# Hybrid decoder layer: the first key projection no longer waits for all of the normalizing, with the lead-in and the whole order of work rearranged

## The chip, the cores and the metric

One core of one Trainium2 chip runs the program. The metric is device time in microseconds (us), the median of several executions. The engines are named as in the profile: PE is the matmul engine TensorE (PEld its weight loads), DVE is VectorE, ACT is ScalarE, POOL is GpSimd, SP is SyncE, which here only issues DMAs.

## The reference

512 tokens of width 1024 get 16 learned meta tokens ahead of them, are normalized and projected. One branch is sliding-window attention, the other RWKV-7 time mixing over 16 heads of 64. Both are gated, added, projected, normalized and passed through a squared-ReLU MLP.

```
h = layer_norm(concat([meta, x]), ln0_g, ln0_b)        # 528 x 1024
proj = h @ w_in                                         # 1024 -> 6656 columns
q, k, v, zr, gate_att, gate_rwkv = split(proj)
att = sliding_window_attention(q, k, v, rel_bias, sinks)
z = zr + (previous token's zr - zr) * shift_mu
r, k, v, wl, al, gl = split(z)
w = -softplus(-(w0 + tanh(wl) @ w2)) - 0.5
a = sigmoid(a0 + al @ a2)
S_t = S w_t + (S (-kk_t)) (kk_t a_t)^T + v_t k_t^T ;  y_t = S_t r_t   # per head, over 528 steps
h = layer_norm(ALPHA h + (sigmoid(gate_att) att + sigmoid(gate_rwkv) rw) @ w_out)
out = layer_norm(ALPHA h + square(relu(h @ w_ff1)) @ w_ff2)[16:]
```

## The kernel before

**Operands.** Activations are kept transposed (features on partitions, tokens along the row) and as two tiles, `hhi` (the value rounded to fp32r) and `hlo` (what is left). Weights are split alike into `whi` (ACT, L656) and `wlo` (DVE, L658). A product is three matmuls, hi by hi, lo by hi, hi by lo (L499, L500, L501). A projection of 128 columns takes eight slices of the 1024 features, so 24 of them for the left half of the tokens (columns 0 to 263) and 24 for the right half (262 to 527).

**Lead-in** (`lead`). Four blocks of 128 tokens, x0 to x3, are loaded into `res` tiles (in the order's rows x0 is `res_125`, x1 `res_126`, x2 `res_127`, x3 `res_128`). Mean and variance of a block come from DVE (`stats`: L773, L776 to L778) or from two sums on ACT (`sums`: L790 to L793); POOL takes the power -0.5 (L781, L794). The block is normalized by DVE (L811) or ACT (L803 and L808). PE transposes two blocks at a time, x0 with x1 and then x2 with x3, in four steps each (L844, sixteen records for two blocks). ACT (L852) or DVE (L856) applies gain and bias, ACT writes `hhi` (L860), DVE or POOL writes `hlo` (L862). The meta rows go the same way on a path of their own: ACT L815, PE L821, DVE L829, L830 and L832, ACT L831. `busy` (L733) puts matmuls of the identity in, whose result nobody reads: twenty ahead of the first transposes and eight ahead of the second, by `WARM`. Two more small things are done by PE there: the transpose of the parameter rows (L751) and the table of relative positions (L903).

**Head.** `head` projects the decay and rate inputs (`COL_WA`, tile `zwa` by L873 and L874), the gate's input (`COL_GL`), the attention's keys and values. `shifted` projects one strip and mixes each token with the one before it (L698 on ACT, L701 on DVE). Then comes a loop over eight pairs of heads: `rwkv(j)`, `attention(j)`, `merge(j)`. In `rwkv`, L958 is the first matmul of a pair. Its key strip is projected, L1032 to L1034 take norms of it, L1076 is the scores, POOL solves 32 x 32 blocks by substitution, and L1191, L1196, L1211 and L1227 are small matmuls of one chain, with copies on ACT (L1200 and L1202) and a transposition on DVE (L1198) between them. L1250, L1254 and L1258 are the same for the meta tokens. L1288 is the chain from chunk to chunk (L1270 and L1273 copy its result back). L1342, L1399 and L1411 belong to the attention.

**Order.** Every operation is registered with its reads and writes, which gives its dependencies. What is issued when on which engine is set by the table `ORDER`, a list of the operations' numbers, and `SLOTS`, the buffers that they get. The costs given to `op` (`wire`, `lag`, `port`, the second argument) are for the search that made the table and do nothing on the chip. An operation `whole` depends on all of the lead-in; every matmul group of a projection made after it names it in `after=late`, and so may stand in the table only behind it. Projections made earlier name the parts they need: `parts_in` gives the transposed slices, `cols_in` the parameter columns.

Of the kernel before, what the change touches and what calls it, by code (L numbers as in the profile page):

```python
# [15 lines left out]
ALU = mybir.AluOpType  # L16
# [4 lines left out]
P = 128  # L21
# [4 lines left out]
T = SEQ + NMETA  # L26
# [8 lines left out]
WARM = (20, 8)  # L35
# [41 lines left out]
for _name, _c in ROWS:  # L77
# [177 lines left out]
]  # L255

def _constants():
# [124 lines left out]
def hybrid_layer_kernel(ctx: ExitStack, tc: tile.TileContext, I: dict, out: bass.AP):  # L382
# [330 lines left out]
    def parts_in(s, end):  # L713
        if late:
            return []
# [1035 lines left out]
```

## Time and profile before

| | |
|---|---|
| median of 3 runs | 923.06 us (922.6 to 924.2) |
| the profiled execution | 924.42 us |
| its span, first to last instruction | 922.6 us |
| instructions | 17014 |
| PE busy | 902.2 us, 98% of the span |
| DVE, ACT, POOL busy | 585.8, 456.3, 245.6 us |
| mean granted clock of PE | 0.994 |

A row of the timeline gives start, length, engine, line, operation, what is written and read, shapes, count, and in brackets the idle time before it with what ended it. A row of waits gives who waited for whom, microseconds in total, times, the longest. A row of windows gives a stretch, its length, the busy time of PE, PEld, DVE, ACT and POOL with the counts, the granted clock, the DMA's share and GB/s. `x34` counts records; one matmul call of the identity leaves two. The busy end of a matmul is modelled, so the step from one start to the next tells more than its length.

### The profile page before, as it was taken

How to read it: one execution, taken by the hardware profiler on the slowest of the kernel's cores; microseconds unless marked ns; L12 is line 12 of the kernel's file. 1: busy time of each engine (PE TensorE's matmuls, PEld its weight loads, DVE VectorE, ACT ScalarE, POOL GpSimd, SP SyncE). 2: the span in 40 equal slices, each digit the busy share in tenths (PEclk: the TensorE clock that was granted, in tenths of full speed). 3: DMA queues.
4: the chain of work that ended last, by engine and by line, in shares of the span. 5: the costliest groups of instructions: out<-in, count | busy, mean ns of one | idle time of the engine just before them, and what ended most of it. 6: DMA issues, size and time to landing. Idle time of an engine off the chain costs nothing. (4 is left out here: it accounts for less than half of the span.)

```text
span 922.6 us, 17014 instructions
## 1 busy us (share of the span) xinstructions
PE 902.2 (98%) x6496; PEld 773.6 (84%) x6496; DVE 585.8 (63%) x1141; ACT 456.3 (49%) x1080; POOL 245.6 (27%) x652
## 2 busy tenths in 40 slices
PE   7999999999999999999999999999999999999996
PEld 6999989888998888978878878888888888888885
DVE  7873977868777696587685887864323244442437
ACT  7845568476583664656637448434312234431120
POOL 4147173381634605507537020000000000000001
PEclk9999999999999999999989999999999999999999
DMA  7443323425242242313246322532223232233322
GB/s 265 125 131 99 93 84 101 111 67 127 72 110 86 68 141 69 83 54 114 64 140 182 100 92 69 172 126 92 92 91 107 76 114 92 91 93 98 100 75 92
DMA packets 71370, 95.90 MB, mean 104 GB/s; under 512 B 40071, under 2 KB 47497, under 8 KB 71289
## 3 DMA queue, kind: packets, MB, share of 16 engines
q1 hardware_dynamic: 70448, 93.65, 33.5%
q8 instruction: 51, 0.84, 0.4%
q10 hardware_dynamic: 840, 1.17, 0.3%
q14 instruction: 31, 0.25, 0.1%
HBM read 87.64 MB, written 8.21 MB: 104 GB/s over the span
## 5 line engine op out<-in xcount | busy, mean ns | idle before, releaser
L499 PE MATMUL g<-hhi,whi 128*128 128x512 f32 (+3 forms) x640 | 213.1, 333 | 0.2
L500 PE MATMUL g<-hlo,whi 128*128 128x512 f32 (+3 forms) x640 | 204.1, 319 | 1.7 <-DVE hlo L862 1.7
L501 PE MATMUL g<-hhi,wlo 128*128 128x512 f32 (+3 forms) x640 | 203.6, 318 | 0.0
L476 ACT CAST whi<-wraw 128x512 fp32r<-128x512 f32 x118 | 67.4, 619 | 205.7 <-PE acc L1616 107.4
L479 DVE TENSOR_TENSOR wlo<-wraw,whi 128x512 fp32r<-128x512 f32 x118 | 76.4, 689 | 144.5 <-ACT whi L476 141.7
L499 PEld LDWEIGHTS g<-hhi,whi 128*128 128x128 f32 x640 | 121.0, 189 | 12.6 <-issue 2.2
L500 PEld LDWEIGHTS g<-hlo,whi 128*128 128x128 f32 x640 | 121.2, 189 | 9.7 <-DVE hlo L862 2.1
L501 PEld LDWEIGHTS g<-hhi,wlo 128*128 128x128 f32 x640 | 121.0, 189 | 8.5 <-DVE wlo L658 0.2
L658 DVE TENSOR_TENSOR wlo<-wraw,whi 128x512 fp32r<-128x512 f32 x126 | 88.3, 708 | 30.4 <-ACT whi L656 29.8
L1167 POOL TENSOR_TENSOR ftmp<-Xf,Nf 108x84 f32<-108x84 f32 (+23 forms) x248 | 88.1, 355 | 73.4 <-DMA Nf<-Nd 44.7
L656 ACT CAST whi<-wraw 128x512 fp32r<-128x512 f32 x126 | 76.9, 618 | 55.5 <-PE g L500 23.5
L466 POOL TENSOR_TENSOR rsf<-rsf,mhalf 128x1 f32<-128x1 f32 x4 | 3.9, 964 | 348.5 <-DVE rsf L465 348.5
L1171 POOL TENSOR_TENSOR Xf<-Xf,ftmp 108x84 f32<-108x84 f32 (+23 forms) x248 | 88.5, 357 | 19.0
L1615 PE MATMUL acc<-wlo,fhi 128*128 128x512 f32 x240 | 93.4, 389 | 0.0
L1614 PE MATMUL acc<-whi,fhi 128*128 128x512 f32 x240 | 93.4, 389 | 0.0
L1616 PE MATMUL acc<-whi,flo 128*128 128x512 f32 x240 | 93.4, 389 | 0.0
L501 PE MATMUL dps<-h1hi,wlo 128*128 128x512 f32 x232 | 91.6, 395 | 0.0
L499 PE MATMUL dps<-h1hi,whi 128*128 128x512 f32 x232 | 91.6, 395 | 0.0
L500 PE MATMUL dps<-h1lo,whi 128*128 128x512 f32 x232 | 91.6, 395 | 0.0
L1614 PEld LDWEIGHTS acc<-whi,fhi 128*128 128x128 f32 x240 | 45.0, 188 | 9.5
L1616 PEld LDWEIGHTS acc<-whi,flo 128*128 128x128 f32 x240 | 45.0, 188 | 9.3
L1615 PEld LDWEIGHTS acc<-wlo,fhi 128*128 128x128 f32 x240 | 45.0, 188 | 9.3
(361 smaller groups left out, 1658.4 us busy)
## 6 DMA issues: line engine op xcount, KB each, us to landing
wraw<-in_w_ff_dram SPq DMA_DIRECT2D x64, 512.0 KB
wraw<-in_w_in_dram SPq DMA_DIRECT2D x52, 512.0 KB
wraw<-in_w_out_dram SPq DMA_DIRECT2D x14, 256.0 KB
Nf<-Nd SPq DMA_DIRECT2D x24, 144.0 KB
res<-in_x_dram SPq DMA_DIRECT2D x4, 512.0 KB
G<-in_consts_dram SPq DMA_DIRECT2D x16, 128.0 KB
XB<-xtd SPq DMA_DIRECT2D x16, 128.0 KB
res<-in_x_dram SPq DMA_DIRECT2D x8, 256.0 KB
```

Source lines behind the costliest of these rows:

```text
L476: act.copy(hi[:n, qs], raw[:n, qs])
L479: dve.tensor_tensor(lo[:n, qs], raw[:n, qs], hi[:n, qs].bitcast(F32), op=ALU.subtract)
L499: pe.matmul(ps, whi, xhi, start=first, stop=False)
L500: pe.matmul(ps, whi, xlo, start=False, stop=False)
L501: pe.matmul(ps, wlo, xhi, start=False, stop=last)
L656: AC(512, lambda hi=hi, qs=qs: act.copy(hi.t, raw.t[:, qs]), plain=True, r=[raw], w=[hi], new=[hi])
L658: f = lambda hi=hi, lo=lo, qs=qs, e=e: e.tensor_tensor(lo.t, raw.t[:, qs], hi.t.bitcast(F32), op=ALU.subtract)
L1167: sub(nj * nt, lambda s=s, nj=nj, nt=nt, tv=tv: pool.tensor_tensor(tv(), Xf.t[:, 0:nj, s : s + 1].to_broadcast([NB, nj, nt]), Nf.t[:, s : ...
L1171: sub(nj * nt, lambda s=s, nj=nj, tv=tv: pool.tensor_tensor(Xf.t[:, 0:nj, s + 1 :], Xf.t[:, 0:nj, s + 1 :], tv(), op=ALU.add), port=1, r=[ ...
L1614: pe.matmul(acc[b], xhi[:, k, bs], hi[:, ws], start=first, stop=False)
L1615: pe.matmul(acc[b], xhi[:, k, bs], lo[:, ws], start=False, stop=False)
L1616: pe.matmul(acc[b], xlo[:, k, bs], hi[:, ws], start=False, stop=last)
```

## The change

The matmuls of the first pair's key projection get the dependencies of a projection made early (the list `early`): the slices of the two halves that they read, not `whole`. Both tables are searched anew over all operations. In the lead-in the work is dealt out differently: x0 is now normalized by ACT and x3 by DVE, x2 is summed by ACT and x1 has its statistics from DVE; half of the low part of the first projection's weights (`COL_WA`) goes from DVE to POOL; there are 16 and 4 identity matmuls instead of 20 and 8; the transposes no longer wait for the identity matmuls ahead of the second half. Some costs that only the search reads are changed too.

```
-WARM = (20, 8)
+WARM = (16, 4)
 ORDER = [
-    0, 1, 26, 2, 3, 127, 5, 128, 4, 67, 30, 29, 27, 131, 68, 6, 34, 69, 7, 36, 8, 28, 42, 243,
...
-    def weights(name, i, qs_=(0, 1)):
+    def weights(name, i, qs_=(0, 1), low=LOW):
...
-            e = (dve, pool)[LOW[q]]
+            e = (dve, pool)[low[q]]
...
-                op("PE", 1394 if n == 512 else 6 * (13 + n / 2.4) - 4, seg, r=[hi, lo, ...] + parts_in(s, t0 + n), ..., after=late)
+                op("PE", 1394 if n == 512 else 6 * (13 + n / 2.4) - 4, seg, r=[hi, lo, ...] + parts_in(s, t0 + n), ..., after=[] if early else late)
...
-        dense("w_in", col // P, spans, evict, [z])
+        dense("w_in", col // P, spans, evict, [z], (0, int(col == COL_WA)))
...
     def parts_in(s, end):
-        if late:
+        if late and not early:
...
     def cols_in():
-        return [] if late else [(bdrv, "omu"), bvc]
+        return [] if late and not early else [(bdrv, "omu"), bvc]
...
-            mean, rs, nm, bmv, brs, bnm = sums(of, P, f"x{b}", list(xb[b])) if b == 1 else stats(of, P, f"x{b}", list(xb[b]))
+            mean, rs, nm, bmv, brs, bnm = sums(of, P, f"x{b}", list(xb[b])) if b == 2 else stats(of, P, f"x{b}", list(xb[b]))
...
-                if b == 3:
+                if b in (0,):
...
-                op("PE", 442, turn, r=src + [bident, (bw, h)], w=[tp] + ([(bw, "h")] if h == 0 else []), new=[tp, full], mode="T")
+                op("PE", 442, turn, r=src + [bident] + ([(bw, 0)] if h == 0 else []), w=[tp] + ([(bw, "h")] if h == 0 else []), new=[tp, full], mode="T")
...
         k = Buf(re_)
+        early.extend([j] if j == 0 else [])
         shifted(COL_K + j * P, 8 + j, k)
+        early.clear()
```

What this does to the order, at three places. Lines of the changed kernel behind L967 are two higher than before (its L1193 is L1191).

On PE, behind the first transposes, before. `res2` and `res3` are blocks x2 and x3:

```order
L821 MATMUL g_115<-con_66,sb0_191 128x16 x8
L903 MATMUL g_116<-bias0_189,relb_102 16x128
L733 MATMUL g_109<-con_66 128x128 x8
L844 MATMUL g_110<-con_66,res2_127 128x128
L844 MATMUL g_110<-con_66,res3_128 128x128
```

Now the first projection follows there (`whi_119` and `wlo_122` are the weights of `COL_WA`):

```order
L844 MATMUL g_116<-con_66,res0_125 128x128
L844 MATMUL g_116<-con_66,res1_126 128x128
L733 MATMUL g_109<-con_66 128x128 x4
L499 MATMUL g_110<-hhi_96,whi_119 128x264
L500 MATMUL g_110<-hlo_97,whi_119 128x264
L501 MATMUL g_110<-hhi_96,wlo_122 128x264
```

After its 24 matmuls come twelve of the first key projection (`whi_120` and `wlo_123`), and only then x2 and x3:

```order
L499 MATMUL g_111<-hhi_96,whi_120 128x264
L500 MATMUL g_111<-hlo_97,whi_120 128x264
L501 MATMUL g_111<-hhi_96,wlo_123 128x264
L844 MATMUL g_112<-con_66,res2_127 128x128
L844 MATMUL g_112<-con_66,res3_128 128x128
```

The left half of the first projection and half of the key's left half have moved ahead of the second transposes; the key's other two quarters stand among and behind them, six matmuls each.

On DVE, the start of the program before (`stx` are statistics, `mvx` mean and variance):

```order
L778 TENSOR_SCALAR nmx_225<-mvx_223 128x1
L811 TENSOR_SCALAR res_125<-res_125,mvx_223,rsx_224 128x512 x2
L773 BN_STATS stx_233<-res_128 128x6 x2
L776 BN_AGGR mvx_234<-stx_233 128x2
L777 TENSOR_SCALAR rsx_235<-mvx_234 128x1
L778 TENSOR_SCALAR nmx_236<-mvx_234 128x1
L811 TENSOR_SCALAR res_126<-res_126,nmx_228,rsx_227 128x512 x2
```

And now:

```order
L778 TENSOR_SCALAR nmx_225<-mvx_223 128x1
L773 BN_STATS stx_226<-res_126 128x6 x2
L776 BN_AGGR mvx_227<-stx_226 128x2
L777 TENSOR_SCALAR rsx_228<-mvx_227 128x1
L778 TENSOR_SCALAR nmx_229<-mvx_227 128x1
L811 TENSOR_SCALAR res_126<-res_126,mvx_227,rsx_228 128x512 x2
L773 BN_STATS stx_233<-res_128 128x6
```

The normalizing of x0 has left DVE, the statistics of x1 have come, and x3's stand behind the normalizing of x1 instead of ahead of it.

On PE, the small chain of the seventh pair, before:

```order
L1191 MATMUL g<-U_184,NT_161 32x32 x16
L1258 MATMUL g<-SVm_165,BTm_171 64x64 x2
L1196 MATMUL g<-XB_180,U_184 32x32 x16
L499 MATMUL g<-hhi,whi 128x266
L500 MATMUL g<-hlo,whi 128x266
L501 MATMUL g<-hhi,wlo 128x266
```

Twelve such wide matmuls stand there, and L1211 behind them. Now:

```order
L1193 MATMUL g<-U_184,NT_161 32x32 x16
L1256 MATMUL g<-RHm_173,XTm_175 16x64 x2
L1198 MATMUL g<-XB_180,U_184 32x32 x16
L1260 MATMUL g<-SVm_165,BTm_171 64x64 x2
L1213 MATMUL g<-AT_177,XB_180 64x128 x16
L499 MATMUL g<-hhi,whi 128x266
L500 MATMUL g<-hlo,whi 128x266
```

The twelve wide matmuls have moved from ahead of L1211 to behind it.

On SP the first DMAs were the meta rows and the four blocks; now they are the meta rows, x0, the sinks, x1, the weights of `COL_WA`, a gate weight, x3, two small ones, the weights of the first key projection, a table and x2.

More of the change, by code (lines that the diff above doesn't have):

```diff
@@ L645, in PO @@
         return op("POOL", cp(n), fn, **k)
-    def weights(name, i, qs_=(0, 1)):
+    def weights(name, i, qs_=(0, 1), low=LOW):
         raw = Buf(rraw)
         part = slice(qs_[0] * 512, (qs_[-1] + 1) * 512)
-        op("SP", 330, lambda: nc.sync.dma_start(raw.t[:, part], I[name][i, :, part]), wire=1325 * len(qs_), w=[raw], new=[raw])
+        op("SP", 330, lambda: nc.sync.dma_start(raw.t[:, part], I[name][i, :, part]), wire=(700 if name == 'w_in' and i in (COL_WA // P, COL_K // P) else 1325) * len(qs_), w=[raw], new=[raw])
         his, los = [], []
@@ L660, in weights @@
             )
-            (DV, PO)[LOW[q]](512, f, port=1, r=[raw, hi], w=[lo], new=[lo])
+            (DV, PO)[low[q]](512, f, port=1, r=[raw, hi], w=[lo], new=[lo])
             his.append(hi)
@@ L664, in weights, with dense @@
         return his, los
-    def dense(name, i, spans, evict, into=()):
-        his, los = weights(name, i)
+    def dense(name, i, spans, evict, into=(), low=LOW):
+        his, los = weights(name, i, low=low)
         for t0, n in spans:
@@ L680, in seg @@
                         )
-                op("PE", 1394 if n == 512 else 6 * (13 + n / 2.4) - 4, seg, r=[hi, lo, (bh, 2 * s), (bh, 2 * s + 1)] + parts_in(s, t0 + n), w=[ps], new=[ps] + (list(into) if t0 == spans[0][0] else []) if s == 0 else [], after=late)
+                op("PE", 1394 if n == 512 else 6 * (13 + n / 2.4) - 4, seg, r=[hi, lo, (bh, 2 * s), (bh, 2 * s + 1)] + parts_in(s, t0 + n), w=[ps], new=[ps] + (list(into) if t0 == spans[0][0] else []) if s == 0 else [], after=[] if early else late)
             evict(ps, t0, n)
@@ L703, in evict @@
                 op0=ALU.mult, op1=ALU.add), r=[ps, (z, t0)], w=[(z, t0)])
-        dense("w_in", col // P, spans, evict, [z])
+        dense("w_in", col // P, spans, evict, [z], (0, int(col == COL_WA)))
     btab, brows, bident, bcon, bbones, brelb, bsink, bl = (Buf(single(None)) for _ in range(8))
     bvc, bdrv, bxtd = (Buf(single(None)) for _ in range(3))
-    late, prepared = [], []
+    late, prepared, early = [], [], []
     tail = Buf(rbias)
     def parts_in(s, end):
-        if late:
+        if late and not early:
             return []
@@ L718, in cols_in @@
     def cols_in():
-        return [] if late else [(bdrv, "omu"), bvc]
+        return [] if late and not early else [(bdrv, "omu"), bvc]
     def lead():
-        op("-", 0, lambda: None, lag=4700, w=[bident])
+        op("-", 0, lambda: None, lag=3300, w=[bident])
         op("-", 0, lambda: None, lag=5200, w=[brows])
@@ L726, in lead @@
         for b in range(4):
-            op("SP", 700, lambda b=b: nc.sync.dma_start(xt[b], I["x"][b * P : (b + 1) * P, :]), wire=2050, w=list(xb[b]), new=list(xb[b]))
+            op("SP", 700, lambda b=b: nc.sync.dma_start(xt[b], I["x"][b * P : (b + 1) * P, :]), wire=1300 if b else 2050, w=list(xb[b]), new=list(xb[b]))
         xmb, zb, fm = Buf(rsb), Buf(rsb), Buf(rbias)
@@ L732, in busy @@
             for i in range(n):
-                op("PE", cost if i < 7 else 230, lambda: pe.matmul(wb.t[:, 0:P], ident, ident, start=True, stop=True), w=[wb, (bw, key)],
+                op("PE", cost if i < 16 else 230, lambda: pe.matmul(wb.t[:, 0:P], ident, ident, start=True, stop=True), w=[wb, (bw, key)],
                    new=[wb] if first and i == 0 else [], **k)
@@ L798, in lead @@
             of = lambda b=b: xt[b]
-            mean, rs, nm, bmv, brs, bnm = sums(of, P, f"x{b}", list(xb[b])) if b == 1 else stats(of, P, f"x{b}", list(xb[b]))
-            minus = ALU.add if b == 1 else ALU.subtract
+            mean, rs, nm, bmv, brs, bnm = sums(of, P, f"x{b}", list(xb[b])) if b == 2 else stats(of, P, f"x{b}", list(xb[b]))
+            minus = ALU.add if b == 2 else ALU.subtract
             moments.append((mean, rs, minus))
-            if b == 3:
+            if b in (0,):
                 op("ACT", 260, lambda nm=nm, rs=rs: act.activation(nm[:, 1:2], nm[:, 0:1], AF.Copy, scale=rs), r=[brs, (bnm, 0)], w=[(bnm, 1)])
@@ L806, in lead @@
                 x = [(xb[b][0], q)] + ([(xb[b][1], q)] if q else [])
-                if b == 3:
+                if b in (0,):
                     AC(512, lambda b=b, qs=qs, nm=nm, rs=rs: act.activation(xt[b][:, qs], xt[b][:, qs], AF.Identity, bias=nm[:, 1:2], scale=rs),
@@ L811, in lead @@
                     op("DVE", 480, lambda b=b, qs=qs, mean=mean, rs=rs, minus=minus: dve.tensor_scalar(
-                        xt[b][:, qs], xt[b][:, qs], mean, rs, op0=minus, op1=ALU.mult), r=[bmv, brs], w=x)
+                        xt[b][:, qs], xt[b][:, qs], mean, rs, op0=minus, op1=ALU.mult), port=1, r=[bmv, brs], w=x)
         mean, rs, nm, bmv, brs, bnm = sums(xm, NMETA, "xm", [xmb])
```

321 rows, old and new, of tables (ORDER, SLOTS) are left out of this document.

## Prediction

> **What bounds the kernel now.** I read the page first, then the stretches of the program, then who made TensorE (PE) wait, and last the first 32 us instruction by instruction.
>
> ```profile
> PE 902.2 (98%) x6496; PEld 773.6 (84%) x6496; DVE 585.8 (63%) x1141; ACT 456.3 (49%) x1080; POOL 245.6 (27%) x652
> 0.00:12.01 12.01, 8.15 (x42) 7.86 (x42) 5.91 (x16) 8.88 (x19) 5.61 (x21) 1.00 0.84 305
> 12.01:20.41 8.40, 6.97 (x61) 6.07 (x59) 7.75 (x17) 7.47 (x15) 3.20 (x3) 1.00 0.65 219
> 20.41:31.48 11.07, 10.83 (x83) 10.27 (x83) 8.79 (x20) 8.26 (x18) 3.61 (x9) 1.00 0.35 126
> 31.48:400.00 368.52, 367.96 (x3403) 329.48 (x3403) 269.71 (x571) 227.97 (x598) 166.62 (x466) 1.00 0.35 97
> 400.00:420.00 20.00, 17.41 (x237) 14.65 (x235) 17.14 (x39) 9.61 (x24) 0.78 (x1) 1.00 0.25 70
> 454.00:464.80 10.80, 8.70 (x117) 6.92 (x116) 10.58 (x25) 3.95 (x12) 1.98 (x9) 1.00 0.46 121
> 464.80:471.60 6.80, 6.17 (x80) 5.36 (x80) 5.69 (x12) 4.14 (x9) 0.64 (x1) 0.50 0.59 171
> ```
>
> The columns after the length are the busy times of PE, PEld, DVE, ACT, POOL, then granted clock, DMA share and GB/s. PE is the bound: from 31.48 to 400 us it idles 0.56 us. A gain can come from three places only: the lead-in (work that is none, up to 31.5 us), the two stretches after 400 us where PE idles, and the 6.8 us in which its clock was granted at half, 3.4 us lost. The waits of PE over the span name the causes:
>
> ```profile
> PE g L733 <- DMA con<-in_consts_dram: 3.1, 1, 3.1
> PE g L1288 <- ACT Z L1273: 2.2, 3, 0.8
> PE g L500 <- DVE hlo L862: 1.7, 2, 1.4
> PE g L1191 <- DVE U L1198: 1.4, 2, 1.2
> PE g L1196 <- ACT U L1200: 0.5, 1, 0.5
> PE g L1032 <- DVE res L701: 0.4, 1, 0.4
> ```
>
> The lead-in on PE (start, length, line; L733 are the idle-time fillers, two records to one call, L844 the transposes, L499 to L501 wide matmuls):
>
> ```profile
> 5.76 6.41 PE L733 MATMUL g<-con 128*128 128x128 f32 x34
> 12.01 1.91 PE L844 MATMUL g<-con,res 128*128 128x128 f32 x16
> 13.85 0.67 PE L821 MATMUL g<-con,sb 16*128 16x16 f32 x8
> 14.44 0.39 PE L903 MATMUL g<-bias,relb 32*16 32x128 f32 x2
> 14.76 2.05 PE L733 MATMUL g<-con 128*128 128x128 f32 x16
> 16.68 2.18 PE L844 MATMUL g<-con,res 128*128 128x128 f32 x16
> 20.41 0.39 PE L500 MATMUL g<-hlo,whi 128*128 128x264 f32 x1 [1.43 <-DVE hlo L862]
> 27.04 0.29 PE L499 MATMUL g<-hhi,whi 128*128 128x264 f32 x1
> 30.67 0.28 PE L499 MATMUL g<-hhi,whi 128*128 128x258 f32 x1
> 31.48 0.70 PE L958 MATMUL g<-zwa,lw 64*128 64x512 f32 x2
> ```
>
> By the order, 30 wide matmuls stand between the rows at 27.04 and 30.67, so one takes 0.121 us, and 84 of them precede L958. The busy PE before 12.01 and from 14.76 to 16.68 does nothing the result needs: PE waits for blocks to be normalized, transposed, scaled and split.
>
> **The change part by part.** New and old both start when the first block of x has landed. These rows give durations on the other engines:
>
> ```profile
> 5.36 1.29 DVE L773 BATCH_NORM_STATS2 stx<-res 128x6 f32<-128x512 f32 x2 [5.36 <-DMA res<-in_x_dram]
> 6.99 0.14 DVE L778 TENSOR_SCALAR nmx<-mvx 128x1 f32<-128x1 f32 x1
> 7.75 1.00 DVE L811 TENSOR_SCALAR res<-res,mvx,rsx 128x512 f32<-128x512 f32 x2 [0.61 <-POOL rsx L781]
> 14.44 0.99 DVE L856 TENSOR_SCALAR e<-g,vc 128x256 f32<-128x256 f32 x2
> 16.54 0.28 DVE L830 TENSOR_TENSOR bias<-bias,vc 128x128 f32<-128x128 f32 x1
> 17.20 1.28 DVE L658 TENSOR_TENSOR wlo<-wraw,whi 128x512 fp32r<-128x512 f32 x2
> 18.40 1.35 DVE L832 TENSOR_TENSOR hlo<-bias,hhi 128x128 fp32r<-128x128 f32 x1
> 9.57 1.24 ACT L815 ACTIVATE sb<-sb,nmxm,rsxm 16x1024 f32<-16x1024 f32 x1
> 11.75 0.81 ACT L808 ACTIVATE res<-res,nmx,rsx 128x512 f32<-128x512 f32 x1
> 13.82 0.56 ACT L852 ACTIVATE e<-g,vc 128x256 f32<-128x256 f32 x1
> 14.27 0.61 ACT L860 CAST hhi<-e 128x512 fp32r<-128x512 f32 x1
> 7.16 0.56 POOL L781 TENSOR_TENSOR rsx<-rsx,mhalf 128x1 f32<-128x1 f32 x1 [0.46 <-DVE nmx L778]
> 18.21 1.40 POOL L862 TENSOR_TENSOR hlo<-e,hhi 128x512 fp32r<-128x512 f32 x1 [1.87 <-ACT hhi L860]
> ```
>
> *First transposes.* Before, DVE normalized block 0, took the statistics of block 3 and only then normalized block 1, so PE started them at 12.01. Now DVE takes both statistics first: 5.36 to 7.13, then the same 1.77 again to 8.9; POOL's power 0.56, to 9.45; the two normalizing halves of block 1, 9.95 and 10.45. ACT takes block 0: after the meta rows (L815, now about 7.0 to 8.25), a bias and one weight cast it reaches L808 at 9.0, two halves, the second done by 10.55. Transposes start at about 10.05, 1.95 earlier. The 16 fillers ahead of them end by then: 34 records took 6.41, thus 0.38 a call, and 16 calls from 3.1 on (PE's first wait, for the constants) with L751 among them end about 9.5; an eighth longer each, 10.3. Then 1.9 of transposes, 0.6 and 0.3 for L821 and L903, 4 fillers instead of 8 (half of 1.92): PE is free at 13.8.
>
> *First wide matmuls.* They need the meta columns (L831, L832) and the first scaled pair. On DVE from 10.45: half of block 3's statistics 0.65, L856 to 12.2, one half of the weight's low part, L829 and L830, L862, the second L856 (to 15.05), L832. The other half of that weight's low part goes to POOL, now about 11.1 to 12.5; I let DVE's half end after it, at 13.1. L832 took 1.35 while POOL ran L862 and 0.28 is what L830 of the same size took; POOL is due to end at 15.0, so I take 0.3, and 1.35 is the far bound. Start: 15.4 (16.4), against 20.41. [...]
>
> *The key projection in the gap.* 24 wide matmuls of the first projection's left half and 12 of the first key projection now stand ahead of the second transposes. They wait once more, for POOL's last piece of blocks 0 and 1. ACT from 10.55: a weight cast, four L852, four L860, L831 and block 2's first sum, with steps 0.1 shorter than the durations (13.82 to 14.27), end about 16.5; POOL's 1.4 behind it gives 18.0. They end at 20.1. Blocks 2 and 3: ACT's second sum of block 2, about as long as the first (1.06 in L790), a weight cast and three small operations end at 18.7, POOL's power at 19.3; DVE normalizes block 3 by 19.65 and block 2 by 20.15 and 20.65. So the transposes go at 20.2 with no real gap, the last two quarters of the key's left half between them, to 23.6. The right halves wait for L862 at 23.75 (0.1) and for POOL's last piece at 27.0 (0.3), and PE comes to L958 at 30.6, where it waits for both activations of zwa, which DVE's and ACT's queues finish about 31.45. There 102 wide matmuls are behind it; before, 84 at 31.48 + 0.27. Gain: 18 x 0.121 + 0.3 = 2.5 us. With L832 at its far bound 2.0; with no DVE wait on POOL at all about 3.0, since the pieces at 18.0 and 27.0 come 0.5 earlier.
>
> *Nothing:* SP's new order. Blocks 0 and 1 stay first:
>
> ```profile
> 6.59 1.06 ACT L790 ACTIVATE GR<-res 128x1024 f32<-128x1024 f32 x1 [0.52 <-DMA res<-in_x_dram]
> ```
>
> Blocks land about 1.25 apart (5.36, 6.6), so the first weight, now third, is there by 8, the key's by 10.7, block 2 (now issued sixth) by 12.3; ACT asks for it at 14.75. If one came 2 us late its cover of 2 us would just be gone.
>
> *The rest of the order.* The same matmuls, 1569 at the end in the same order. Two places differ on the seventh pair:
>
> ```profile
> 465.59 1.06 PE L1196 MATMUL g<-XB,U 32*32 32x32 f32 x32 [0.52 <-ACT U L1200]
> 401.57 1.21 PE L1211 MATMUL g<-AT,XB 64*64 64x128 f32 x32 [0.34 <-DVE pown L1404]
> ```
>
> The 12 wide matmuls that covered ACT's copy between L1196 and L1211 now follow L1211. With only L1258 as cover, L1196 waited 0.52 behind such a copy and L1211 of the pair before 0.34: +0.4. L1411's eight, which stood between L1034 and L1076, go ahead of L1062: they cover the 0.4 of L1032 and uncover up to as much at L1076: 0. The three waits at L1288 keep their bare links: 0. Unknown small waits, both signs: -0.1, bounds -1 to +1.2. Sum +0.3.
>
> Total -2.5 + 0.3 = -2.2 us. The profiled execution took 924.42 (span 922.6 and 1.8 around it); it would take 922.2. The median is 1.36 lower, 923.06; so 920.9. The halved clock I keep at 3.4 us, since the stretch of small matmuls and short waits ahead of it stays.
>
> **The rivals.** About 0.2% (1.85 us) is what a measurement of this kernel can tell: 921.2 and 924.9 are the bounds.
>
> *One: the clock stays whole.* It fell after 10.8 us of small matmuls with 2.1 us idle. If the shifted stretch is just above what halves it, 3.4 us go: 917.5. Against it: the stretch gains a wait. Chance 0.13.
>
> *Two, slower: the clock is halved a second time,* at L1196 to L1211 of the sixth pair or in the new gap of PE from 13.8 to 15.4, each as short of matmuls as the stretch at 454. Price 3.4: 924.3, and 925 with the far bounds of the sum. [...] For it: 400 to 420 already idles 2.6 us. Against it: that stretch kept its clock. Chance 0.16. [...]
>
> *Three: the head start is swallowed.* The change would not do what it says if the key's matmuls only replace fillers while the second transposes slip by as much: from 16.68 to 20.2 they do slip 3.5. If DVE and ACT, over 80% busy there (7.75 and 7.47 of 8.40), run 2 us later than I laid them, 923.1. Chance 0.10.
>
> *Rest:* 0.08 for other waits after 31 us, mostly dearer.
>
> **How the numbers follow.** Forecast 920.9, chance 0.53, own range 919.1 to 922.3 (2.0 to 3.0 gained in the lead-in, -1 to +1.2 behind it); two thirds of it lie under 921.2. Faster: 0.34 + 0.13 + 0.03 = 0.50. Same: 0.19 + 0.10 + 0.07 of rival two = 0.36. Slower: 0.09 + 0.05 = 0.14. The range runs from rival one to rival two, 917.5 to 924.4, with half of each and of the rest outside.
>
> **What would show it.** First L844 at 10.0 to 10.3; L500 going on at 15.4 to 16.4; second L844 near 20.2; L958 near 31 with 102 wide matmuls done; one stretch at clock 0.50 near 463 to 471. Wrong: first L500 after 17, two such stretches or none, or PE idle above 4 us in 454 to 475 (2.7 now by two of the rows above).

## The result, and the profile after

| | before | changed |
|---|---|---|
| median beside each other | 924.52 us (12 runs, 922.6 to 926.19) | 928.85 us (12 runs, 926.26 to 932.52) |
| the profiled execution | 924.42 us | 932.07 us |
| its span, mean granted clock of PE | 922.6 us, 0.994 | 930.3 us, 0.983 |

The ratio is 1.0052 (95% interval 1.0036 to 1.0068): 0.5% slower, where the prediction had 0.23% faster and a range that ended at 924.4. Two single executions far above all others, of two kernels below (1780.87 and 2255.51 us), are left out of every comparison.

The same views as before, now of the changed kernel. First its TensorE (PE) line and the stretches, cut at the same places of the program: up to the first transposes, up to the second ones, up to L958 of the first pair, then the plain middle and the two stretches behind 400 us.

```profile
PE 909.7 (98%) x6480; PEld 778.6 (84%) x6480; DVE 583.7 (63%) x1140; ACT 455.1 (49%) x1080; POOL 246.1 (26%) x653
...
0.00:11.14 11.14, 6.31 (x33) 6.12 (x33) 3.70 (x11) 7.41 (x15) 4.47 (x20) 1.00 0.70 247
11.14:24.28 13.14, 12.90 (x70) 11.93 (x71) 10.48 (x23) 9.53 (x22) 6.45 (x13) 0.61 0.68 235
24.28:34.80 10.52, 10.41 (x84) 9.92 (x82) 8.96 (x19) 7.35 (x16) 2.80 (x2) 1.00 0.37 122
34.80:400.00 365.20, 364.79 (x3338) 326.36 (x3339) 265.55 (x563) 226.32 (x594) 165.62 (x457) 1.00 0.35 97
400.00:420.00 20.00, 17.86 (x233) 14.89 (x228) 14.50 (x33) 8.05 (x21) 1.63 (x9) 0.86 0.22 68
454.00:465.45 11.45, 11.26 (x89) 9.16 (x87) 11.25 (x24) 6.50 (x17) 1.41 (x8) 1.00 0.31 74
465.45:479.10 13.65, 11.02 (x133) 8.69 (x134) 12.45 (x28) 4.80 (x12) 1.98 (x8) 0.63 0.52 143
```

PE is busy 7.5 us longer with 16 records fewer: matmuls got longer, not more. The column that tells why is the granted clock, third from the end: 0.61, 0.86 and 0.63 in three stretches, where before only 6.8 us near 465 us stood at 0.50. The middle idles 0.4 us, before 0.6. Over the whole span PE idles 20.6 us (930.3 less 909.7), before 20.4: what this execution loses lies in longer matmuls and not in added waits.

The waits of PE, the largest over the whole span:

```profile
PE g L733 <- DMA con<-in_consts_dram: 3.1, 1, 3.1
PE g L1290 <- ACT Z L1275: 2.5, 4, 0.9
PE g L844 <- ACT res L808: 1.8, 1, 1.8
PE g L1344 <- DVE NT L1086: 1.2, 1, 1.2
PE g L1193 <- DVE U L1200: 0.7, 2, 0.6
PE g L1198 <- ACT U L1202: 0.6, 1, 0.6
```

The wait for `hlo` of L862 (1.7) is gone. PE now waits 1.8 us ahead of the first transposes, and in the seventh pair L1344 (the attention's scores) waits 1.2 us for VectorE (DVE). It reads nothing of `NT`; going by the kernel's operands, what it waits for is the bank that it writes. There the wait of the small chain's first matmuls has shrunk from 1.4 (L1191) to 0.7 (L1193). The lead-in, from PE's, DVE's, ScalarE's (ACT) and SyncE's (SP) timelines:

```profile
6.42 2.97 PE L733 MATMUL g<-con 128*128 128x128 f32 x18
11.14 0.33 PE L844 MATMUL g<-con,res 128*128 128x128 f32 x1 [1.75 <-ACT res L808]
18.21 0.57 PE L499 MATMUL g<-hhi,whi 128*128 128x264 f32 x1
18.58 0.42 PE L500 MATMUL g<-hlo,whi 128*128 128x264 f32 x1
24.28 1.47 PE L844 MATMUL g<-con,res 128*128 128x128 f32 x12
34.82 0.69 PE L958 MATMUL g<-zwa,lw 64*128 64x512 f32 x1
```

```profile
8.48 1.29 DVE L773 BATCH_NORM_STATS2 stx<-res 128x6 f32<-128x512 f32 x2 [1.55 <-DMA res<-in_x_dram]
```

```profile
9.76 0.62 ACT L656 CAST whi<-wraw 128x512 fp32r<-128x512 f32 x1 [1.20 <-DMA wraw<-in_w_in_dram]
10.28 1.51 ACT L808 ACTIVATE res<-res,nmx,rsx 128x512 f32<-128x512 f32 x2
```

```profile
1.64 0.43 SPq L744 DMA_DIRECT2D sinks<-in_attn_sinks_dram  x1
```

Block x1 lands at 8.48, not at 6.6, and the first weight at 9.76, not by 8. ACT's queue stands in the weight's cast, and behind it is the normalizing of x0 that the transposes need. The fillers had ended at 9.38. And SP had put the broadcast of the sinks (16 numbers to 128 partitions, L744) between x0 and x1, where the old order has it at 14.27.

### The profile page after: what moved, and what is told of

It reads as the page before. It is cut to its first block, busy times and chain, and to the rows that moved or that the text cites. A ratio compares the mean times of both kernels' runs of the same rounds, so it can differ in the third digit from the quotient of the medians.

```text
span 930.3 us, 16970 instructions
## 1 busy us (share of the span) xinstructions
PE 909.7 (98%) x6480; PEld 778.6 (84%) x6480; DVE 583.7 (63%) x1140; ACT 455.1 (49%) x1080; POOL 246.1 (26%) x653
## 4 chain that ended last, share of the span: by engine, by line
PE 86%; DVE 7%; POOL 3%; ACT 2%; issue 1%; DMA 1%; SPq 0%; DVEq 0%; POOLq 0%; ACTq 0%
PE g L499 10%; PE g L500 10%; PE g L501 10%; PE acc L1617 6%; PE acc L1618 6%; PE acc L1616 6%; PE dps L499 6%; PE dps L500 6%; PE dps L501 6%; PE g L1229 2%; PE g L1078 2%; PE g L1290 1%; PE g L1413 1%; PE g L1344 1%; PE g L1465 1%
## 5 line engine op out<-in xcount | busy, mean ns | idle before, releaser
L500 PE MATMUL g<-hlo,whi 128*128 128x512 f32 (+3 forms) x640 | 205.2, 321 | 0.1
L479 DVE TENSOR_TENSOR wlo<-wraw,whi 128x512 fp32r<-128x512 f32 x118 | 76.4, 688 | 144.0 <-ACT whi L476 143.8
L499 PEld LDWEIGHTS g<-hhi,whi 128*128 128x128 f32 x640 | 122.0, 191 | 11.5 <-issue 1.9
L500 PEld LDWEIGHTS g<-hlo,whi 128*128 128x128 f32 x640 | 122.1, 191 | 7.7 <-POOL hlo L862 0.3
L658 DVE TENSOR_TENSOR wlo<-wraw,whi 128x512 fp32r<-128x512 f32 x125 | 86.4, 703 | 30.3 <-ACT whi L656 27.2
L1169 POOL TENSOR_TENSOR ftmp<-Xf,Nf 108x84 f32<-108x84 f32 (+23 forms) x248 | 85.8, 346 | 71.3 <-DMA Nf<-Nd 33.3
L656 ACT CAST whi<-wraw 128x512 fp32r<-128x512 f32 x126 | 77.1, 618 | 44.0 <-PE g L500 20.2
L1173 POOL TENSOR_TENSOR Xf<-Xf,ftmp 108x84 f32<-108x84 f32 (+23 forms) x248 | 91.6, 369 | 18.3
L500 PE MATMUL dps<-h1lo,whi 128*128 128x512 f32 x232 | 91.6, 395 | 0.0
L1275 ACT ACTIVATE Z<-g,PC 64x64 f32<-64x64 f32 x64 | 19.8, 309 | 69.1 <-DVE Z L1272 33.9
```

The source lines that it names most:

```text
L479: dve.tensor_tensor(lo[:n, qs], raw[:n, qs], hi[:n, qs].bitcast(F32), op=ALU.subtract)
L499: pe.matmul(ps, whi, xhi, start=first, stop=False)
L500: pe.matmul(ps, whi, xlo, start=False, stop=False)
L656: AC(512, lambda hi=hi, qs=qs: act.copy(hi.t, raw.t[:, qs]), plain=True, r=[raw], w=[hi], new=[hi])
L658: f = lambda hi=hi, lo=lo, qs=qs, e=e: e.tensor_tensor(lo.t, raw.t[:, qs], hi.t.bitcast(F32), op=ALU.subtract)
L1169: sub(nj * nt, lambda s=s, nj=nj, nt=nt, tv=tv: pool.tensor_tensor(tv(), Xf.t[:, 0:nj, s : s + 1].to_broadcast([NB, nj, nt]), Nf.t[:, s : ...
```

## The experiments

Each kernel was timed in turn with the kernel before (its median, of the executions beside them, in brackets) and profiled once. Theory one is about the lead-in: the broadcast ahead of x1, and the idle time and half clock it brings. Theory two: behind the fifth pair the new order itself loses, mostly through a halved clock, and a head start would last.

**1. More fillers.** The last filler of the first group becomes nine (`for _ in range(9 if key == 0 and i == n - 1 else 1)`).

> The changed kernel with eight more filler matmuls behind the last one of the first group, so that TensorE stays busy from 9.4 to about 11.2 us. Theory one (the idle 1.75 us ahead of the first L844 brought the half clock of the lead-in): the clock stays whole from 8.1 us on, the first wide matmuls at 18 to 22 us run at 0.11 to 0.12 us a step and not 0.22, and 1 to 2 us are won: 927 to 928. Rival (the lead-in is bound by the landings of x1 and of the first weight and by VectorE, whatever the clock): clock whole, but under 0.5 us won: 928.3 to 929. Second rival (the clock falls for other reasons): half clock in the lead-in all the same, no change.

930.12 us (before 924.12), ratio 1.0058 (1.0042 to 1.0073), clock 0.985 to 0.988 in the timed executions. Nothing was won, and the time lies above the ranges of theory one and of the rival. Its own trace is of a left-out execution, so whether its lead-in ran at full clock isn't known, and the two rivals aren't told apart.

**2. The broadcast late.** One number moves in the table:

```
-    0, 1, 22, 2, 27, 119, 3, 120, 123, 6, 853, 63, 5, 7, 8, 26, 9, 64, 532, 65, 10, 235, 11, 25,
-    37, 4, 12, 66, 38, 33, 67, 550, 13, 34, 356, 39, 14, ...
+    0, 1, 22, 2, 119, 3, 120, 123, 6, 853, 63, 5, 7, 8, 26, 9, 64, 532, 65, 10, 235, 11, 25, 37,
+    4, 12, 66, 38, 33, 67, 550, 13, 34, 356, 39, 27, 14, ...
```

> The changed kernel with the sinks' broadcast issued behind the lora's first slice (about 10 us), and nothing else moved. Theory one (the broadcast ahead of x1 all but stops the transfers from 4.2 to 6 us): no such hole, x1 lands near 6.6 and not 8.5 us, the first weight near 8 and not 9.75, the first L844 is at 9.8 to 10.4 and not 11.1, and 1.5 to 4 us are won, 925 to 927.4, the more the less the clock falls. Rival (the hole has another cause, as the two gate weights of 64 KB each): the hole stays, x1 at 8.5 us, no change. Second rival (x1 is early, but what sets the lead-in's end is VectorE and ScalarE behind it): x1 early, under 0.5 us won.

The lead-in did what the prediction had laid out. PE's timeline of this kernel:

```profile
9.96 1.67 PE L844 MATMUL g<-con,res 128*128 128x128 f32 x12
...
15.49 0.39 PE L500 MATMUL g<-hlo,whi 128*128 128x264 f32 x1 [0.89 <-DVE hlo L832]
...
20.14 1.53 PE L844 MATMUL g<-con,res 128*128 128x128 f32 x12
...
30.75 0.69 PE L958 MATMUL g<-zwa,lw 64*128 64x512 f32 x1
```

Forecast were 10.05, 15.4, 20.2 and "near 31" (31.45 in the working); 102 wide matmuls stand before the last row. What the broadcast does shows in the rates of the first 12 us, 40 slices of 0.3 us, of the changed kernel and of this one:

```profile
GB/s 0 0 0 0 0 96 145 253 116 148 396 410 410 342 69 16 46 46 44 125 180 275 315 369 437 423 399 406 428 442 358 444 374 408 429 383 431 389 399 430
```

```profile
GB/s 0 0 0 0 0 68 164 275 237 118 266 297 427 399 394 417 369 382 396 396 410 437 343 398 391 435 399 393 400 416 408 428 352 362 454 393 444 381 339 286
```

From 4.2 to 6.0 us all engines together moved 16 to 125 GB/s, where 369 to 417 went without the broadcast. Yet the time is 929.03 us (924.12), ratio 1.0050 (1.0033 to 1.0067), within the interval of the changed kernel. That is the outcome of the second rival, but not its mechanism: the end of the lead-in did come earlier (L958 at 30.75 against 34.82). The head start is there and doesn't arrive.

**3. Both**, with four more fillers.

> Both: the broadcast late, and four more filler matmuls to bridge 9.4 to 10.2 us. Theory one (the lead-in lost what was forecast to these two, and the rest has its own loss): the second group of L844 near 20 to 21.5 us and not 24.3, L958 of the first pair near 31 and not 34.8, 3 to 4.5 us won, 924.4 to 926, so level with the kernel before or up to 1.5 us behind it, since the pairs at 400 to 475 us still cost 4 to 5 us more than before. Rival (the lead-in is the whole loss): 921 to 923. Second rival (the lead-in has no part in it): 928 to 929.

928.5 us, ratio 1.0040 (1.0021 to 1.0060). The lead-in was as in the kernel above (first and second L844 at 10.06 and 20.24), the total 2.5 us above theory one's range and where the rival had it that gives the lead-in no part. The lead-in is not the whole loss, nor most of it.

**4. The broadcast early, in the kernel before** (its operation 31 behind operation 2, nothing else).

> The kernel before with nothing but the sinks' broadcast put at the place that the change gives it, between x0 and x1. Theory one (the broadcast stops the queue): a hole of near 1.8 us in the transfers at 4 to 6 us, x1 and what is behind it 1.5 to 2 us later, the first L844 1 to 2 us after 12.0 us, 0.5 to 2 us slower: 925 to 926.5. Rival (the hole has another cause): no hole, no change, 924.5. Second rival (hole, but x1 has slack in the kernel before): hole, no change.

927.2 us (924.12), ratio 1.0030 (1.0016 to 1.0043): 3 us for one 8 KB transfer, more than theory one's bound. The hole is there, and the first transposes wait for block x1:

```profile
GB/s 0 0 0 0 0 82 147 214 292 75 138 398 367 418 249 50 61 17 2 45 84 302 396 437 396 410 410 410 423 396 437 437 377 372 425 417 437 382 413 410
```

```profile
10.69 0.27 PE L844 MATMUL g<-con,res 128*128 128x128 f32 x1
12.46 1.86 PE L844 MATMUL g<-con,res 128*128 128x128 f32 x15 [1.50 <-DVE res L811]
```

They go on 0.45 us later than the 12.01 of before, and the fifth pair's L1191 starts 0.9 later (335.0 against 334.1). What is above that goes with the clock: there is a halved window at 336.1 that the profiled execution of the kernel before didn't have, and the median clock of the timed executions was 0.992 against 0.994. Why the clock falls there is not shown.

**5. The changed kernel again,** with three kernels beside it.

> The changed kernel itself, so that the next three have it on their own chip. All theories: 927.5 to 930.5, half clock behind some window of 3.41 us with TensorE busy for under 0.7 of it, at 400 to 421 and 463 to 473 us at least.

930.11 us (924.37), ratio 1.0059 (1.0046 to 1.0071), clock 0.985 to 0.989. This execution's lead-in was not halved (L958 at 32.39), and still it lost 8 us behind the fifth pair.

Where each profiled execution stands, by the start of the first matmul of a group (us); halved stretches but for the last few us of each:

| | fifth pair's L1193 | sixth pair's first link | seventh pair's L1193 | eighth pair's first link | last matmul | clock 0.50 at (length) |
|---|---|---|---|---|---|---|
| before | 334.1 | 407.8 | 463.6 | 532.6 | 914.2 | 464.8 (6.8) |
| changed | 335.4 | 411.7 | 469.5 | 539.7 | 921.7 | 11.5 (10.2), 404.0 (3.4), 417.7 (3.4), 468.9 (10.2) |
| changed again | 333.0 | 410.5 | 469.2 | 539.3 | 921.1 | 335.3 (6.8), 417.2 (6.8), 468.4 (10.2) |
| broadcast late | 331.4 | 406.2 | 464.5 | 534.4 | 916.6 | 411.9 (3.4), 463.1 (10.2) |
| head_old_rest_new | 334.9 | 409.8 | 466.3 | 536.0 | 917.8 | 464.3 (10.2) |
| head_new_rest_old | 333.7 | 407.4 | 463.2 | 532.4 | 914.0 | 465.2 (6.8) |
| joint_822 | 334.1 | 410.7 | 466.5 | 535.6 | 917.1 | 34.7 (3.4), 335.1 (6.8), 468.2 (6.8) |

With the broadcast late the changed order is 2.7 us ahead at the fifth pair (331.4 against 334.1), 0.9 behind at the seventh and 2.4 behind at the end. The head start is lost between the fifth and the eighth pair; behind that the distances grow by at most 0.6 us.

The table also bounds what the clock cost. Behind the fifth pair's L1193 and ahead of the last few us, the changed kernel ran 17.0 and 23.9 us at half clock, the kernel before 6.8. Half of the difference, 5.1 and 8.5 us, is the most that this can have cost (an estimate: a wide matmul's step was 0.22 us at half clock and 0.12 at full, behind 18.58 and behind 21.82 in the changed kernel); the two lost 6.2 and 8.0 us there. The timed executions agree. Of 18 of the changed kernel the two granted 0.992 took 926.26 and 926.82 us; of 115 of the kernel before, beside runs 1 to 9, the 17 at 0.992 have a median of 925.88. At equal clock the changed kernel is less than 1 us behind. But its median clock is 0.987, that of the kernel before 0.994.

In these traces the clock changes in steps of 3.41 us: ahead of the last few us, the changed kernel's halved stretches are 10.24, 3.41, 3.41 and 10.24 us long, and the starts of the other three lie 115, 119 and 134 times 3.413 us behind the first. The rows below are cut by such steps, and windows of 3.41 us in what follows are cut so too. Of the changed kernel, the windows at the two falls that belong to its links (414.25) and to the seventh pair (465.45), and what followed each:

```profile
414.25:417.66 3.41, 1.77 (x10) 1.26 (x9) 2.86 (x7) 1.32 (x4) 0.00 (x0) 1.00 0.36 81
417.66:421.08 3.42, 2.76 (x8) 1.97 (x6) 2.06 (x6) 0.98 (x3) 0.00 (x0) 0.50 0.40 145
...
465.45:468.86 3.41, 2.20 (x13) 1.19 (x12) 3.24 (x9) 0.87 (x2) 0.80 (x5) 1.00 0.37 85
468.86:472.27 3.41, 2.05 (x55) 1.64 (x56) 3.32 (x9) 1.48 (x5) 0.00 (x0) 0.50 0.44 112
```

The kernel before at the same places of the program:

```profile
410.23:413.64 3.41, 2.70 (x14) 2.21 (x15) 2.10 (x6) 1.82 (x4) 0.00 (x0) 1.00 0.33 63
...
461.42:464.84 3.42, 2.02 (x47) 1.36 (x43) 3.29 (x9) 0.30 (x2) 0.00 (x0) 1.00 0.66 173
```

Its links leave PE 2.70 us of work in the window and keep the clock; the changed ones leave 1.77. The old order puts six wide matmuls each between the fourth and fifth and the fifth and sixth link; the new one moves the first six up between the second and third, and the two waits that follow, 0.93 and 0.71 us, fall into one window with little else. The other traces bear this out. Six profiled executions have the new order of links without fillers there, with 1.77 to 1.84 us of work in the sparsest window of the links; in five of them the clock fell behind it. Seven have the old order without fillers, with 1.99 us or more; in none did it fall there. At the seventh pair the clock is halved for 10.2 us in all five with the new order and no fillers in it, and for 6.8 us in six of seven with the old one.

**6. Fillers in the waits of the sixth and seventh pair,** 19 for the changed kernel and for the one with the late broadcast, 12 for the kernel before: `pe.matmul(t, ident, ident, start=True, stop=True)` at the start of `inv3`, `inv4`, `fold_w`, `link`, and behind `meta0`, for those two pairs.

> The changed kernel with idle TensorE time of 400 to 475 us filled with dummy matmuls of 128x128 (0.24 us each at full clock) in the sixth and seventh pair, inside waits that the trace of the changed kernel shows: two ahead of each L1193 group, one and two ahead of L1198, one ahead of L1213, four behind L1242, three, two and two ahead of the links of L1290 that wait 0.93, 0.71 and 0.71 us. Theory two (behind the lead-in the new order loses by the half clock that follows sparse windows): no or one half stretch of 3.4 us there, stretched matmuls of 0 to 3 us and not 9.8, total 922.5 to 925.5, 4 to 6 us under the changed kernel. Rival (the new order loses by its waits, the half clock only lies beside them): waits as before, 0 to 1.5 us slower than the changed kernel, 928 to 930.

> The kernel before with dummy matmuls at its own waits of 408 to 417 and 461 to 466 us: four ahead of L1191 of the seventh pair, two ahead of its L1196, two ahead of each of the three links of the sixth pair that wait 0.7 us. Theory two: its half stretch near 465 us goes, 2 to 4 us won, 920.5 to 922.5. Rival: 0 to 1 us slower, 924 to 925.5.

> The changed kernel with both mended: the broadcast late and the waits of the sixth and seventh pair filled. If the lead-in's 4 us and the half clock behind it are the whole of the miss: head start of 2.5 to 3 us over the kernel before up to the fifth pair, kept through the seventh; 918.5 to 921.5. If the fillers don't hold the clock: 926 to 929, as with the broadcast alone. If the new order has a loss of its own beside the clock: 922 to 925.

929.36 us (ratio 1.0049, 1.0037 to 1.0061), 925.47 (1.0014, 1.0005 to 1.0023) and 928.33 (1.0047, 1.0035 to 1.0060), before 924.37. The first two lie in the rival's ranges. The third lies where it was expected if the fillers don't hold the clock, but they held it (0.990 to 0.996); it is 3.3 us above the range for a loss beside the clock. The clock did rise: 0.993 to 0.997 in the timed executions of the first, against 0.985 to 0.989 of the changed kernel beside it. The time did not follow. Most of the fillers wrote a bank that was still being read, and so stood behind the waits instead of in them, as in the third kernel's links (L1186 is the filler, L1299 the link):

```profile
412.91 0.94 PE L1186 MATMUL g<-con 128*128 128x128 f32 x6 [0.92 <-ACT Z L1283]
413.68 0.39 PE L1299 MATMUL g<-Z,G 128*128 128x128 f32 x2
```

19 times 0.24 us (eight calls of the identity took 1.92 in the kernel before, 14.76 to 16.68) is 4.6 us, which may be what the clock brought. The kernel before lets this be estimated: its 115 timed executions lie about a line of 0.89 us for each thousandth of the clock. Its twelve fillers cost 2.9 us by their length and raised its median clock from 0.994 to 0.996, worth 1.8 us; the difference is 1.1 us, as measured. So these runs are inconclusive on theory two: they changed two things at once.

**7. Fillers meant to stand in the waits:** eight for the seventh pair as above, with `inv4`'s two in a bank that nobody reads; two ahead of the last link of the sixth pair; and the six wide matmuls between its second and third link moved one link on (operation 2418 behind 2063).

> The changed kernel with its waits of the sixth and seventh pair truly covered, where the dummy matmuls of the earlier run stood behind the waits and cost their time: in the sixth pair the six wide matmuls that lie between the second and third link go one link later, into the wait of 0.93 us, and two dummies of 0.24 us go ahead of the last link into a bank that nobody reads; in the seventh pair four dummies behind L1242, two ahead of L1193, two ahead of L1198 into a free bank. Theory two (half clock behind sparse windows is the loss): at most 3.4 us of half clock in 400 to 475 us in most runs, 2 to 5 us under the changed kernel, 924 to 927. Rival (the fillers cost what the clock brings): 928 to 930.

> The same with the broadcast late as well. Theory two, with the head start of the lead-in: 920 to 924, level with the kernel before or up to 4 us ahead of it. Rival: 926 to 929 as with the broadcast alone.

> The broadcast late, and only the seventh pair covered. Theory two: half clock near 408 to 415 us stays in most runs (3.4 us), that near 463 to 473 us goes or shrinks to 3.4 us: between the broadcast alone (929) and both pairs covered, 923 to 927. Rival: 926 to 929.

> The kernel before with two dummies ahead of each of its three waiting links of the sixth pair, into a bank that nobody reads, and four ahead of L1191 of the seventh. Theory two: its half clock at 465 us goes or shrinks, 1 to 3 us won, 921.5 to 923.5. Rival: 924 to 925.5.

929.25 us (ratio 1.0043, 1.0027 to 1.0059), 927.19 (1.0029, 1.0018 to 1.0039), 927.6 (1.0044, 1.0031 to 1.0057) and 924.33 (1.0002, 0.9988 to 1.0016); before 924.25. All four again lie in the rival's ranges. With the broadcast late and fillers in both pairs the kernel is still 3 us behind the kernel before at nearly its clock (0.992 to 0.994 in ten of twelve timed executions). So this way doesn't win the time back, and theory two falls as it was put. It does not clear the clock: ten fillers cost 2.4 us by their length, and not all waits were covered. In the three changed kernels the two fillers of `inv4` waited 0.95 us themselves, and where the six wide matmuls had moved, two links still waited 1.0 and 0.7 us. In the profiled executions of those two kernels the clock did not fall at the links. The runs don't say which part of the order loses; the next do.

**8. Two orders joined.** The tables of both kernels were cut at one operation and joined: the first n operations of one order, the remaining ones in the order of the other; a buffer whose place is taken at the joint gets another.

> The changed kernel with the broadcast late, its order up to the second pair's inverse (the first 925 of 3079 operations, about 165 us) and from there the remaining operations in the order of the kernel before, with buffers given anew where the joint asks for it. Theory two (the new order loses behind the fifth pair): the head start of 2 to 3 us stays to the end, half clock there as in the kernel before (6.8 us near 462 us): 920.5 to 923. Rival (the head start is worth nothing, whatever follows it): 924 to 925.5. Second rival (the joint's own waits): over 925.5.

> The same, cut right behind the lead-in (187 operations, about 18 us). Theory two: 920.5 to 923.5, if the old order can use the head start. Rival: 924 to 925.5.

> The kernel before up to about 210 us (1168 of its 3087 operations), and from there the order of the changed kernel; nothing of the new lead-in is in it. Theory two: no head start, and the loss of the sixth and seventh pair as in the changed kernel, 3 to 7 us slower than the kernel before: 927.5 to 931. Rival (the loss sits in the new lead-in and what follows from it): 924 to 925.5.

> As the first, cut at about 165 us, but with the broadcast ahead of x1 as the changed kernel has it. Theory one (the broadcast there costs 1.5 to 3 us in the changed kernel too): 1.5 to 3 us slower than the first, 923 to 925.5. Rival (in the changed kernel the broadcast costs nothing): level with the first.

| | median (before 924.29) | ratio, interval |
|---|---|---|
| head_new_rest_old | 924.28 | 1.0002 (0.9990 to 1.0013) |
| lead_new_rest_old | 925.92 | 1.0020 (1.0009 to 1.0031) |
| head_old_rest_new | 930.62 | 1.0067 (1.0051 to 1.0084) |
| head_new_sinks_first | 926.23 | 1.0024 (1.0013 to 1.0035) |

This settles where the loss is. The new order from 210 us on, with nothing of the new lead-in, costs 6.3 us, more than the whole change: that half of theory two is shown. Up to 0.8 us of it belongs to the joint: so much is gone at the fifth pair (334.9 against 334.1), where PE waits twice for 0.4 us that it doesn't wait for in the kernel before. The other half of theory two fell: joined at 165 us, the new lead-in with the old rest costs nothing and brings nothing, as its rival had it. Joined right behind the lead-in it costs 1.6 us, above its rival's range; there PE waits 1.4 and 0.7 us for DVE (L1041 and L1351 there) behind the joint. The broadcast ahead of x1 costs 1.95 us (926.23 against 924.28), less than in run 4. Of head_old_rest_new, the window ahead of its fall and the stretch behind it, and the wait that opens it:

```profile
460.90:464.31 3.41, 2.18 (x23) 1.40 (x19) 3.30 (x9) 0.87 (x2) 1.63 (x9) 1.00 0.02 5
464.31:474.55 10.24, 9.57 (x123) 7.62 (x124) 9.45 (x21) 3.93 (x10) 0.18 (x1) 0.50 0.64 185
```

```profile
PE g L1349 <- DVE NT L1091: 1.2, 1, 1.2
```

(Its L1349 is the changed kernel's L1344.) DVE is busy 3.30 of 3.41 us there: PE waits for an engine that has no time left. That was so before too (3.29 of 3.42 us), and PE's larger waits from about 400 us to the end of the seventh pair add up to 4.9 us here, to 5.6 in the changed kernel and to 5.1 in the kernel before: they moved more than they grew. The six times of head_old_rest_new go with their clocks, 927.68 at 0.992 to 932.40 at 0.985; a line through them gives 0.62 us for each thousandth, against 0.89 in the kernel before. From its median 0.989 to the 0.994 of the kernel before that makes 3.1 to 4.5 of the 6.3 us. The remaining 1.9 to 3.2 us, with the joint's 0.8 in them, are not traced to a place. That split is an estimate.

**9. Other joints,** since the one at 165 us gave the head start away by itself: PE waited there for DVE at L1229 (L1227 before).

```profile
PE g L1236 <- DVE G L1095: 0.9, 2, 0.6
```

(L1236 there.)

> The changed kernel with the broadcast late, its order up to operation 822 (about 150 us), then the remaining ones in the order of the kernel before. Theory two (only the order behind the fifth pair loses, the head start itself lasts): 2 to 2.5 us ahead of the kernel before at the fifth pair's inverse and at the end, 921.5 to 923. Rival (whatever runs the old rest falls back into its pace, since VectorE and ScalarE had work put off behind the head start): under 0.7 us ahead from the third pair on, 923.7 to 925.

> The same, joined at operation 312 (about 60 us). Theory two: 921.5 to 923.5. Rival: 923.7 to 925.5.

924.29 us (before 924.73), ratio 0.9991 (0.9982 to 1.0001), and 924.86, ratio 1.0000 (0.9989 to 1.0011). At the fifth pair they stood 0.0 (its clock had been halved at 34.7) and 1.3 us ahead. Both times lie in their rivals' ranges, but joint_312's lead is larger than the 0.7 us that the rival's mechanism allows. At equal clock joint_822 is ahead: six executions at 0.992 have a median of 924.48 us, three of the kernel before 925.75; four at 0.994 have 923.0, thirteen of the kernel before 924.6. So at equal clock 1.3 to 1.6 us of the head start last, by these few executions; its median clock, 0.992 against 0.994, takes most of that. No version was shown to beat the kernel before; what the head start is worth to a rest that fits it stays open between nothing and 1.7 us, the far end of joint_822's interval.

## Why the prediction was wrong, point by point

- **The step that failed is "The rest of the order", summed to +0.3 us, with the halved clock held at 3.4 us beside it.** It measured about +6: head_old_rest_new has that part alone (6.3 us, up to 0.8 of it the joint's), and between the fifth pair and the last matmul the two profiled executions of the changed kernel took 586.3 and 588.1 us, the old one 580.1. The prediction compared the order at two places of the seventh pair, found a lost cover of 0.4 us at L1211, and let the rest cancel. As a sum of waits that came out nearly right: PE's idle time from 454 to 475 us, where growth above 4 us was to show an error, stayed at 2.8 and 2.6 us (2.7 before). The waits were others: L1213 of the seventh pair went without one, and the attention's scores waited 1.2 us while L1193 waited less than L1191 had. What the sum had no term for is the clock that these shifts cost. The links kept bare waits, as it said, but the six wide matmuls that had moved between them left two of these waits in one window. Bounds of -1 to +1.2 were put on a table in which every row had moved.
- **"The halved clock I keep at 3.4 us, since the stretch of small matmuls and short waits ahead of it stays."** The stretch stayed, and the clock was halved for 17 us behind 400 us in both executions of the changed kernel against 6.8: up to 5.1 us more lost (an estimate). That is rival two's mechanism. It named the sixth pair, L1196 to L1211, where the clock fell at 404.0 in one execution; in both it fell at the links too, near 417. The rival had one more halving, priced at 3.4 us, and 0.16 as its chance.
- **"*Nothing:* SP's new order."** The step looked at which block is issued before which, and passed over a transfer of 8 KB between x0 and x1. It cost 1.95 us in the joined kernels and 3 in the old one. Its sentence "If one came 2 us late its cover of 2 us would just be gone" holds for x2 alone. In the prediction's own times x1 lands at 6.6 and DVE asks for it at 7.13, a cover of 0.5 us. x1 and the weight came 1.9 and 1.8 late, and DVE and ACT waited 1.55 and 1.20 us for them.
- **The lead-in, -2.5 us:** right in mechanism and size once that transfer is out of the way. The first three times came within 0.1 us, L958 0.7 ahead of the working's 31.45, and at the fifth pair the gain was 2.7. With the transfer in the way it was 1.1 in one execution, and -1.3 in the other, whose clock was halved from 11.5 us; in both the first L500 came after 17 us (18.58 and 17.25), one of the prediction's signs of being wrong. That VectorE's half of the first weight's low part (L658) has to end behind POOL's, which the working puts at 13.1, is shown by no run: with the broadcast late it ran from 12.22 to 13.02, and in the changed kernel from 14.49, 0.68 us long, with POOL's half done at 13.65.
- **Rival three (head start swallowed), 0.10:** the second transposes didn't slip, as it had them; the head start was swallowed all the same, far behind the lead-in with the clock, or at a joint, where PE waits for DVE.
- **Rival one (clock whole):** no profiled execution showed it.
- **What the falls follow** is shown in part. The fall at 417.66 follows waits of 0.93 and 0.71 us, 1.64 of 3.41 us without work. Every halved stretch but the last of an execution is 3.41, 6.83 or 10.24 us long, one to three of the steps above. In 19 profiled executions, of 45 windows of one step at full clock with PE busy below 2.45 us 19 were followed by a halved one, of about 240 between 2.45 and 3.3 us 14, of about 4600 above that 10; the two bounds were chosen afterwards. Which sparse window is followed by a fall differs from run to run, and the ten behind busy windows, all of them near 31 and 331 us, are unexplained.

## What to carry to other kernels

A table that a search has rewritten as a whole is to be compared stage by stage on every engine, above all in the stages where another engine is the bound: here six wide matmuls that moved up by two links were followed by a halved clock, for 3.4 us or more, in five of six profiled executions, and the sum of waits didn't show it. When a kernel's executions differ in granted clock, compare those at equal clock too: it shows how much of a loss goes with the clock. Of a load queue, the smallest transfer counts too (one of 8 KB cost 1.95 and 3 us here): look for what stands between the two loads that the first work needs. And when an edit shows its forecast in the trace and not in the time, join the halves of the two versions: it tells which half loses, if the waits at the joint are looked at.

## What was not expected of the hardware

- One broadcast of 64 bytes to 128 partitions, 8 KB, all but stopped the transfers for about 1.8 us (2 to 125 GB/s against about 400) in both kernels above that have it between the first large loads.
- A thousandth of the mean clock goes with 0.6 to 0.9 us of this program's time (0.62 by the six executions of head_old_rest_new, 0.89 by 115 of the kernel before). The mean clock differed by 0.007 between executions of head_old_rest_new, and its time by 4.7 us.
- Dummy matmuls raised the changed kernel's clock to 0.993 and more (0.985 to 0.989 without them) and hardly shortened it (929.36 us against 930.11): 19 of 0.24 us are 4.6 us, and the six thousandths of clock may have brought 3.7 to 5.3 at 0.62 to 0.89 us each (an estimate). Those that wrote a bank whose readers weren't done stood behind the wait that they were to fill: 0.92 us idle ahead of L1186 in the third kernel of run 6, where the changed kernel's link had waited 0.93.
